# The recurrence of a hybrid transformer layer taken one direction at a time, with its input projection first

## The chip, the cores and the metric

The kernel runs on one core of a Trainium2 chip. Its engines are TensorE (PE, matmuls), VectorE (DVE), ScalarE (ACT), GpSimd (POOL) and SyncE (SP, which issues transfers); each works its own row of instructions in order, and the engines meet at semaphores. The metric is the device time of one execution in microseconds, the median of several runs.

## What is computed

Two transformer layers over 1024 latent tokens and 256 context tokens, 1024 channels wide. Layer 0 is a convolution module beside windowed attention, layer 1, which the change touches, is a bidirectional gated linear recurrence (RG-LRU) beside latent attention (MLA); a gated feed-forward follows each. Layer 1's mixer begins so:

```python
    xb_l, gt_l, cq_l, ckv_l, kr_l = split(hl @ w_in)     # recurrence, gate, query, key/value, rope key
    xb_c, gt_c, cq_c, ckv_c, kr_c = split(hc @ w_in)
    hf_l, hf_c = rglru_direction(xb_l, xb_c, ..., False) # forward
    hb_l, hb_c = rglru_direction(xb_l, xb_c, ..., True)  # backward
    c_l = ((hf_l + hb_l) * jax.nn.gelu(gt_l.astype(jnp.float32))).astype(hl.dtype)
    ...
        xc = dwconv(u, conv_w, conv_b, pad[0], pad[1])   # inside a direction: 4 taps
        r = jax.nn.sigmoid(block_diag(xc, gate_w[0], gate_b[0]).astype(jnp.float32))
        i = jax.nn.sigmoid(block_diag(xc, gate_w[1], gate_b[1]).astype(jnp.float32))
        log_a = -LRU_C * r * neg_sp
        bx = jnp.sqrt(-jnp.expm1(2.0 * log_a)) * i * xc.astype(jnp.float32)
        return jnp.exp(log_a), bx
```

Then a linear scan h = a h + bx over the context and, from its last state, over the latent tokens. `cq` and `ckv` go through an RMS norm before their own projections.

## The kernel before

Every float32 matmul is made of three passes over a high and a low part of each operand (`gemm`, L310 to 318: L315 hh x wh, L316 hl x wh, L317 hh x wl). Over 1024 input channels that is 8 k-tiles, so 24 matmuls for 128 output channels and one group of tokens: groups g0 and g1 are 512 latent tokens each, g2 the 256 context tokens. A weight tile is loaded by SyncE, its high part cast by ScalarE (L295, `wh`), its low part subtracted by GpSimd or VectorE (L298, `wl`).

The stage of the change is `proj1`, layer 1's input projections. It runs over the letters of `PROJ1` in their order: "x" projects the recurrence's input (four channel tiles on g0 and g1, then the four on g2), "c" the queries' compressed form (3 tiles), "k" the keys' and values' (2 tiles, three groups), "g" the gate branch (4 tiles, through gelu), "r" the rope key. After each gemm `pump(us)` advances the side programs in `flows` by as much of their own counting as the gemm is worth; a side program is a generator, and each `yield` of a number says for how long it rests. The order of each engine's row comes from that, and from the framework's scheduler behind it. `drain(key)` runs the side programs of one kind to their end at that place. `normed`, used by "c" and "k", starts with `drain("nrm")`, projects, and spawns a side program `fin` that takes each group's norm (matmuls with a ones vector at L436, a reciprocal root by eleven short VectorE steps L440 to 445, the diagonal `dg` at L452, a broadcast matmul at L457) and scales the columns (L1123).

The recurrence is the side program `lru` (L995 to 1065). It goes over the four channel tiles; `todo` tells it that a tile's input is written. For a tile it makes the convolution (`taps`: `xb` is read back from memory, L1013 and three L1017 for each direction, tiles of 128 x 1283), then for both directions twelve gate matmuls (L1035) with a sigmoid each (L1036), the input gate's product on GpSimd (L1038), tanh, exp and square on ScalarE (L1041, L1047, L1050), a product on VectorE (L1051), the square root on ScalarE (L1054), and then on VectorE a product (L1057) and the two scans (L1059 context, L1061 latent) of each direction. GpSimd adds the two directions (L1063) and SyncE writes the sum out (`hsd`). The numbers `LY` say how long the side program rests between these steps. ScalarE holds the tables of one set of functions; ACT_TABLE_LOAD is the change from one to another (sigmoid, exp, sqrt, gelu are in different ones here).

After `proj1` comes `mla`, the latent attention: it splits the normed columns (L321, L322), fills the constant tiles `va` and `gd` on GpSimd (L1258 to 1262), copies the rope key's tiles (L219, `kh`, `kl`, `kc`), splits the first key weights (`wk`, L1282), and starts the value gemms (L1274 to 1276) and key gemms.

Of the kernel before, what the change touches and what calls it, by code (L numbers as in the profile page):

```python
# [13 lines left out]
AF = mybir.ActivationFunctionType  # L14
ALU = mybir.AluOpType
# [10 lines left out]
TOK = (512, 512, 256)  # L26
# [34 lines left out]
PACE = 2.3  # L61
N0 = "SG"
QE0 = "VGG"
LY = (2.0, 1.0, 1.0, 2.0, 1.0, 1.0)
GY = 30.0, 4.0
DH = "s"
DL = "s"
QE00 = "GVV"
KE = "VV"
LY0 = 10.0  # L70
PROJ1 = "cxkgr"
ORD0 = "BABABABABB"

PO1 = (), ("n+++++nn",)
# [24 lines left out]
def tile_backbone(ctx: ExitStack, tc: tile.TileContext, a: dict, out: bass.AP):  # L99
    nc = tc.nc  # L100
    V, S, G, T = nc.vector, nc.scalar, nc.gpsimd, nc.tensor
    DQ = {"s": nc.sync, "a": nc.scalar, "g": nc.gpsimd}
# [20 lines left out]
    def nm(s):  # L123
        uid[0] += 1
        return f"{s}{uid[0]}"
# [10 lines left out]
    def wide():  # L136
        return psum["ca"].tile([128, 1536], F32, tag="ca", name=nm("ca"))
# [17 lines left out]
    def gate(bi, after):  # L155
        if after is not None:
            tc.add_manual_dep(bi.ins, after.ins.name, mybir.DependencyInfo(mybir.DependencyClass.NoSync, mybir.DependencyReason.DATA), reason="order")
        return bi
# [39 lines left out]
    def bank():  # L198
        return psum["mm"].tile([128, 512], F32, tag="mm", name=nm("mm"))
# [61 lines left out]
    for r, items in enumerate(rows):  # L261
        n = 0
# [17 lines left out]
    def cols(key, i, n=1):  # L280
        r, o = at[key]
        return C[:, r, o + i:o + i + n]
# [668 lines left out]
    hsd = drp.tile([128, 4, 1024], F32, name="hsd")  # L951
# [4 lines left out]
    XW = 1024 + 3 + 256  # L956
# [38 lines left out]
    def lru(todo, x5, GW, sp, tiny, done):  # L995
        def seg(t, g):
            o = OFF[g] + (3 if g == 2 else 0)
            return t[:, o:o + TOK[g]]

        def taps(i):  # L1000
            XB = x5("xb", 1)
            for o in (0, 1027, 1286):
                G.memset(XB[:, o:o + 3], 0.0)
            nc.sync.dma_start(XB[:, 3:1027], xbd[:, i, 0:1024])
            nc.sync.dma_start(XB[:, 1030:1286], xbd[:, i, 1024:1280])
            yield 3.0
            XC = []
            for d in range(2):
                x = x5("xc", 4)[:, 0:XW]
                XC.append(x)  # L1010
                tap = lambda k: cols("lcw", (d * 4 + k) * 4 + i)
                A = wide()[:, 0:XW]
                V.tensor_scalar(A, XB[:, 3:3 + XW], tap(0 if d else 3), cols("lcb", d * 4 + i), ALU.mult, ALU.add)  # L1013
                ks = (1, 2, 3) if d else (0, 1, 2)
                for k in ks:
                    o = k + 3 if d else k
                    V.scalar_tensor_tensor(x if k == ks[-1] else A, XB[:, o:o + XW], tap(k), A, ALU.mult, ALU.add)  # L1017
            return XC

        XN = None  # L1020
        for i in range(4):
            while i not in todo:
                yield 2.0
            XC = XN if XN is not None else (yield from taps(i))
            XN = None
            yield LY0 if i == 0 else LY[0]
            R, I, TT = ([x5(n, 2)[:, 0:XW] for _ in range(2)] for n in ("r", "i", "tt"))
            for d in range(2):
                x = XC[d]
                for dst in (R[d], I[d]):  # L1030
                    V.memset(dst[:, 1024:1027], 0.0)  # L1031
                for q, dst in ((0, R[d]), (1, I[d])):
                    for g in range(3):
                        ps = bank()[:, 0:TOK[g]]
                        T.matmul(ps, GW[d][:, q * 4 + i], seg(x, g), start=True, stop=True)  # L1035
                        last = S.activation(seg(dst, g), ps, AF.Sigmoid, bias=cols("lgb", (d * 2 + q) * 4 + i))  # L1036
                    yield LY[1]
                G.tensor_mul(I[d], I[d], x)  # L1038
            for d in range(2):
                c0 = d * 4 + i  # L1040
                last = gate(S.activation(TT[d], R[d], AF.Tanh, scale=sp[:, 0, c0:c0 + 1]), last)  # L1041
            if i + 1 in todo:
                XN = yield from taps(i + 1)
            yield LY[2]
            for d in range(2):
                c0 = d * 4 + i
                gate(S.activation(R[d], R[d], AF.Exp, scale=sp[:, 1, c0:c0 + 1]), last)  # L1047
            A2 = XC
            for d in range(2):
                last = S.activation(A2[d], R[d], AF.Square)  # L1050
                V.scalar_tensor_tensor(TT[d], A2[d], 1.0, TT[d], ALU.add, ALU.mult)  # L1051
            yield LY[3]
            for d in range(2):
                gate(S.activation(TT[d], TT[d], AF.Sqrt, bias=tiny), last)  # L1054
            yield LY[4]
            for d in range(2):
                V.tensor_mul(TT[d], TT[d], I[d])  # L1057
                st = (lambda t, p, q: t[:, p:q][:, ::-1]) if d else (lambda t, p, q: t[:, p:q])
                V.tensor_tensor_scan(st(A2[d], 1027, XW), st(R[d], 1027, XW), st(TT[d], 1027, XW), 0.0, ALU.mult, ALU.add)  # L1059
                init = A2[d][:, 1027:1028] if d else A2[d][:, XW - 1:XW]  # L1060
                V.tensor_tensor_scan(st(A2[d], 0, 1024), st(R[d], 0, 1024), st(TT[d], 0, 1024), init, ALU.mult, ALU.add)  # L1061
                yield LY[5]
            G.tensor_add(A2[0][:, 0:1024], A2[0][:, 0:1024], A2[1][:, 0:1024])  # L1063
            DQ[DH].dma_start(hsd[:, i], A2[0][:, 0:1024])
            done(i, "h")

    def mixer1(hs, nxt):
        pc = ph[0]
# [26 lines left out]
    def proj1(hs, w, pa, tab, KR, wv):  # L1095
# [49 lines left out]
        ready, todo = {}, set()  # L1145
        GW, sp, tiny = lru_setup(pa)
        spawn(lru(todo, x5, GW, sp, tiny, gated), "lru")
        def p_xb():
            for gs in ((0, 1), (2,)):
# [56 lines left out]

        for p in PROJ1:
            {"x": p_xb, "c": p_cq, "k": p_kv, "r": p_kr, "g": p_gt}[p]()
# [618 lines left out]
```

## Time and profile before

| | |
|---|---|
| median of 3 runs | 3096.5 us (3095.42 to 3097.85) |
| profiled execution | 3100.69 us |
| its span, first to last instruction | 3098.9 us |
| mean granted TensorE clock | 0.974 |
| TensorE busy | 2942.0 us (95%) |
| VectorE busy | 1747.0 us (56%) |
| ScalarE busy | 1093.4 us (35%) |
| GpSimd busy | 990.6 us (32%) |
| first projection gemm of layer 1 to the last | 1585.5 to 1828.9 us |

The profile holds one execution. A row of a timeline gives start and length in us, engine, line of the code, operation, the tile written and those read, and in brackets the idle time ahead of it with what ended it. TensorE's clock is given as the share of full speed that was granted.

### The profile page before, as it was taken

How to read it: one execution, taken by the hardware profiler on the slowest of the kernel's cores; microseconds unless marked ns; L12 is line 12 of the kernel's file. 1: busy time of each engine (PE TensorE's matmuls, PEld its weight loads, DVE VectorE, ACT ScalarE, POOL GpSimd, SP SyncE). 2: the span in 40 equal slices, each digit the busy share in tenths (PEclk: the TensorE clock that was granted, in tenths of full speed). 3: DMA queues.
4: the chain of work that ended last, by engine and by line, in shares of the span. 5: the costliest groups of instructions: out<-in, count | busy, mean ns of one | idle time of the engine just before them, and what ended most of it. 6: DMA issues, size and time to landing. Idle time of an engine off the chain costs nothing. (4 is left out here: it accounts for less than half of the span.)

```text
span 3098.9 us, 37481 instructions
## 1 busy us (share of the span) xinstructions
PE 2942.0 (95%) x14441; PEld 2356.5 (76%) x14441; DVE 1747.0 (56%) x2631; ACT 1093.4 (35%) x1631; POOL 990.6 (32%) x730
## 2 busy tenths in 40 slices
PE   7997899899999999999999889999998999999998
PEld 4886777778888888889997556666686888888886
DVE  4799883665654455568545986667355132232234
ACT  4213884532221112145433763333344222111213
POOL 4676546821110011055432341110253222112223
PEclk8998999999999999999999899999998999999999
DMA  8343113434442344269744230010152121111212
GB/s 295 119 129 100 37 34 111 147 101 129 139 136 82 116 144 145 88 195 281 246 155 152 94 111 26 31 38 28 57 160 89 48 62 55 34 41 55 61 41 109
DMA packets 330768, 327.04 MB, mean 106 GB/s; under 512 B 27121, under 2 KB 280734, under 8 KB 330590
## 3 DMA queue, kind: packets, MB, share of 16 engines
q1 hardware_dynamic: 326784, 321.74, 32.3%
q10 hardware_dynamic: 3806, 2.91, 0.3%
q8 instruction: 113, 1.85, 0.2%
q14 instruction: 65, 0.53, 0.1%
HBM read 255.36 MB, written 69.21 MB: 105 GB/s over the span
## 5 line engine op out<-in xcount | busy, mean ns | idle before, releaser
L298 POOL TENSOR_TENSOR wl<-wr,wh 128x1024 fp32r<-128x1024 f32 x154 | 379.9, 2468 | 1314.2 <-ACT wh L295 1283.1
L295 ACT CAST wh<-wr 128x1024 fp32r<-128x1024 f32 x248 | 259.9, 1049 | 1072.3 <-PE big L316 682.3
L315 PE MATMUL big<-hh,wh 128*128 128x512 f32 x1376 | 541.2, 394 | 4.9 <-DVE ga L1485 2.6
L316 PE MATMUL big<-hl,wh 128*128 128x512 f32 x1376 | 538.6, 392 | 3.1 <-POOL hl L503 3.1
L317 PE MATMUL big<-hh,wl 128*128 128x512 f32 x1376 | 538.8, 392 | 0.6 <-DVE wl L298 0.6
L315 PE MATMUL mm<-hh,wh 128*128 128x256 f32 (+1 forms) x1000 | 346.0, 346 | 9.6 <-DVE i L1031 9.5
L316 PE MATMUL mm<-hl,wh 128*128 128x256 f32 (+1 forms) x1000 | 339.0, 339 | 4.0 <-POOL hl L503 2.0
L317 PE MATMUL mm<-hh,wl 128*128 128x256 f32 (+1 forms) x1000 | 338.0, 338 | 3.2 <-POOL wl L298 2.5
L315 PEld LDWEIGHTS big<-hh,wh 128*128 128x128 f32 x1376 | 260.7, 190 | 61.9 <-ACT hh L498 3.4
L316 PEld LDWEIGHTS big<-hl,wh 128*128 128x128 f32 x1376 | 260.4, 189 | 58.9 <-POOL hl L503 4.3
L317 PEld LDWEIGHTS big<-hh,wl 128*128 128x128 f32 x1376 | 260.5, 189 | 55.6 <-DVE wl L298 1.0
L1553 PE MATMUL mm<-zh,wh 128*128 128x512 f32 x704 | 276.6, 393 | 1.2 <-ACT xt L1656 0.7
L1554 PE MATMUL mm<-zl,wh 128*128 128x512 f32 x704 | 275.0, 391 | 0.3 <-DVE zl L322 0.3
L1555 PE MATMUL mm<-zh,wl 128*128 128x512 f32 x704 | 275.2, 391 | 0.0
L1560 DVE TENSOR_TENSOR acc<-acc,mm 128x512 f32<-128x512 f32 x224 | 150.5, 684 | 178.7 <-PE mm L1555 178.5
L473 POOL TENSOR_TENSOR sq<-t,sq 128x512 f32<-128x512 f32 (+1 forms) x153 | 194.8, 1276 | 170.2 <-ACT t L469 152.0
L1485 DVE SCALAR_TENSOR_TENSOR ga<-big,C,ga 128x1023 f32<-128x1023 f32 x86 | 110.2, 1281 | 235.1 <-ACT ga L1498 233.8
L315 PEld LDWEIGHTS mm<-hh,wh 128*128 128x128 f32 x1000 | 192.3, 192 | 35.7 <-DVE i L1031 9.9
L316 PEld LDWEIGHTS mm<-hl,wh 128*128 128x128 f32 x1000 | 191.9, 192 | 29.4 <-POOL hl L503 5.0
L317 PEld LDWEIGHTS mm<-hh,wl 128*128 128x128 f32 x1000 | 191.6, 192 | 24.3 <-POOL wl L298 3.3
L398 DVE SCALAR_TENSOR_TENSOR wa<-wm,sc,wa 128x256 f32<-128x256 f32 x280 | 148.9, 556 | 90.4 <-DMA wm<-in_w_mod_dram 87.6
L298 DVE TENSOR_TENSOR wl<-wr,wh 128x1024 fp32r<-128x1024 f32 x94 | 131.5, 1399 | 111.6 <-ACT wh L295 108.6
(350 smaller groups left out, 5278.5 us busy)
## 6 DMA issues: line engine op xcount, KB each, us to landing
wr<-in_ffn_w_up_dram SPq DMA_DIRECT2D x132, 512.0 KB, 4.3
wm<-in_w_mod_dram SPq DMA_DIRECT2D x224, 128.0 KB, 2.2
wr<-in_ffn_w_down_dram SPq DMA_DIRECT2D x44, 512.0 KB, 3.5
wm<-in_w_mod_dram SPq DMA_DIRECT2D x40, 512.0 KB, 6.5
xd<-x SPq DMA_DIRECT2D x38, 512.0 KB, 4.1
x<-xd SPq DMA_DIRECT2D x38, 512.0 KB, 6.6
wr<-in_ab_w_out_dram SPq DMA_DIRECT2D x24, 512.0 KB, 7.2
wdd<-wh SPq DMA_DIRECT2D x22, 512.0 KB, 2.6
```

What stands on the lines that cost most here:

```text
L295: S.copy(hi[:, 0:nk, 0:m], raw[:, 0:nk, 0:m])
L298: (G if e[wn[0] % len(e)] == "G" else V).tensor_sub(lo[:, 0:nk, 0:m], raw[:, 0:nk, 0:m], f32(hi[:, 0:nk, 0:m]))
L315: T.matmul(ps, wh, xh[k], start=i == 0, stop=False)
L316: T.matmul(ps, wh, xl[k], start=False, stop=False)
L317: T.matmul(ps, wl, xh[k], start=False, stop=i == n - 1)
L398: V.scalar_tensor_tensor(acc[:, v], raw, sc[:, k, v:v + 1], acc[:, v], ALU.mult, ALU.add)
L473: self.eng.tensor_add(self.acc[-1], t, self.acc[-1])
L1485: V.scalar_tensor_tensor(dst[:, lo:hi], src[:, lo + d - o:hi + d - o], k, dst[:, lo:hi], ALU.mult, ALU.add)
L1553: T.matmul(ps, wh, zh, start=j == j0, stop=False)
L1554: T.matmul(ps, wh, zl, start=False, stop=False)
L1555: T.matmul(ps, wl, zh, start=False, stop=j == j1 - 1)
L1560: V.tensor_add(ys[g][c], ys[g][c], ps)
```

## The change

The unit of `lru` becomes one direction of one channel tile: eight units u, tile u // 2, direction u % 2. `gates(u)` holds the gate matmuls, sigmoids, GpSimd's product and the tanh of a unit; `ahead(i)` the taps of a tile. Unit u goes exp, square, product, then the gates of unit u + 1, then its square root, product and scans. `r`, `i` and `tt` still have two buffers, which are now those of two units, not of two directions. GpSimd's add and the write follow each second unit. `LY` gets new numbers, and `PROJ1` puts x ahead of c: "xckgr".

```diff
-LY = (2.0, 1.0, 1.0, 2.0, 1.0, 1.0)
+LY = (2.0, 2.0, 1.0, 2.0, 3.0, 3.0)
...
-PROJ1 = "cxkgr"
+PROJ1 = "xckgr"
...
-            for d in range(2):
-                c0 = d * 4 + i
-                last = gate(S.activation(TT[d], R[d], AF.Tanh, scale=sp[:, 0, c0:c0 + 1]), last)
-            if i + 1 in todo:
-                XN = yield from taps(i + 1)
-            yield LY[2]
-            for d in range(2):
-                c0 = d * 4 + i
-                gate(S.activation(R[d], R[d], AF.Exp, scale=sp[:, 1, c0:c0 + 1]), last)
-            A2 = XC
-            for d in range(2):
-                last = S.activation(A2[d], R[d], AF.Square)
-                V.scalar_tensor_tensor(TT[d], A2[d], 1.0, TT[d], ALU.add, ALU.mult)
-            yield LY[3]
-            for d in range(2):
-                gate(S.activation(TT[d], TT[d], AF.Sqrt, bias=tiny), last)
...
+        def gates(u):
+            i, d = u // 2, u % 2
+            R, I, TT = RI[u] = [x5(n, 2)[:, 0:XW] for n in ("r", "i", "tt")]
+            x, c0 = XC[i][d], d * 4 + i
+            for q, dst in ((0, R), (1, I)):
+                V.memset(dst[:, 1024:1027], 0.0)
+                for g in range(3):
+                    ps = bank()[:, 0:TOK[g]]
+                    T.matmul(ps, GW[d][:, q * 4 + i], seg(x, g), start=True, stop=True)
+                    last[0] = gate(S.activation(seg(dst, g), ps, AF.Sigmoid, bias=cols("lgb", (d * 2 + q) * 4 + i)), last[0] if g == q == 0 else None)
+                yield LY[1]
+            G.tensor_mul(I, I, x)
+            last[0] = S.activation(TT, R, AF.Tanh, scale=sp[:, 0, c0:c0 + 1])
...
+        yield from ahead(0)
+        yield LY0
+        yield from gates(0)
+        for u in range(8):
+            i, d = u // 2, u % 2
+            (R, I, TT), A2, c0 = RI[u], XC[i][d], d * 4 + i
+            gate(S.activation(R, R, AF.Exp, scale=sp[:, 1, c0:c0 + 1]), last[0])
+            last[0] = S.activation(A2, R, AF.Square)
+            V.scalar_tensor_tensor(TT, A2, 1.0, TT, ALU.add, ALU.mult)
+            yield LY[0]
+            if u < 7:
+                yield from gates(u + 1)
+            last[0] = gate(S.activation(TT, TT, AF.Sqrt, bias=tiny), last[0])
             yield LY[4]
...
+            if d:
+                h = XC[i][0][:, 0:1024]
+                G.tensor_add(h, h, A2[:, 0:1024])
+                DQ[DH].dma_start(hsd[:, i], h)
+                done(i, "h")
+            elif i < 3:
+                yield from ahead(i + 1)
```

`gate(x, y)` only puts x behind y in the order of their engine. Lines behind L1066 stand 3 further on in the changed kernel, and lines inside `lru` have new numbers: the gate matmul is L1031, its sigmoid L1032, the product on GpSimd L1034, tanh L1035, exp L1048, square L1049, VectorE's products L1050 and L1056, the square root L1054, the scans L1058 and L1060, GpSimd's add L1064. The number of instructions is the same on every engine but ScalarE, which has 14 more table loads (40 instead of 26).

TensorE, at the norms of c. Before (the norm of c's g0, between two gemms of x; `mm_14014` and `dg_14029` are the context norm):

```order
L317 MATMUL mm_13989<-hh_11736,wl_13986 128x512
L436 MATMUL mm_14014<-ones,sq_13863 128x1 x2
L436 MATMUL mm_14031<-ones,sq_13747 128x1 x4
L315 MATMUL mm_14053<-hh_12595,wh_13985 128x512
...
L317 MATMUL mm_14053<-hh_12598,wl_13986 128x512
L457 MATMUL mm_14078<-dg_14029,ones 128x256
L457 MATMUL mm_14093<-dg_14048,ones 128x512
L315 MATMUL mm_14116<-hh_11733,wh_14112 128x512
```

After (both norms of c, ahead of k's first gemm `mm_14617`):

```order
L1031 MATMUL mm_14533<-xc_14470,gw_13668 128x512
L1031 MATMUL mm_14536<-xc_14470,gw_13668 128x256
L436 MATMUL mm_14545<-ones,sq_14276 128x1 x4
L457 MATMUL mm_14564<-dg_14562,ones 128x512
L436 MATMUL mm_14578<-ones,sq_14334 128x1 x4
L457 MATMUL mm_14597<-dg_14595,ones 128x512
L315 MATMUL mm_14617<-hh_11733,wh_14613 128x512
```

Before, a gemm of 24 matmuls stands between a norm's column sums and its broadcast; after, none does for c's norms. For k's first norm (`dg_14944`) one gemm and three gate matmuls stand there after.

VectorE, the steps of such a norm up to its `dg`. Before (k's first norm, among g's gemms, the one that TensorE waits for in rows 3 below):

```order
L445 SCALAR_TENSOR_TENSOR rst_14899<-mm_14894,rst_14899 128x4
L1013 TENSOR_SCALAR ca_15080<-xb_15073,C 128x1283
L1051 SCALAR_TENSOR_TENSOR tt_14756<-xc_14693,tt_14756 128x1283
L1051 SCALAR_TENSOR_TENSOR tt_14757<-xc_14699,tt_14757 128x1283
L443 TENSOR_TENSOR mm_14894<-mm_14894,rst_14899 128x4
L1017 SCALAR_TENSOR_TENSOR ca_15080<-xb_15073,C,ca_15080 128x1283
L444 SCALAR_TENSOR_TENSOR mm_14894<-mm_14894,rst_14899 128x4
L1017 SCALAR_TENSOR_TENSOR ca_15080<-xb_15073,C,ca_15080 128x1283
L445 SCALAR_TENSOR_TENSOR rst_14899<-mm_14894,rst_14899 128x4
L1057 TENSOR_TENSOR tt_14756<-tt_14756,i_14754 128x1283
L452 TENSOR_TENSOR dg_14911<-ident,rst_14899 128x512
```

After (c's second norm; `xc_14815` takes over a buffer that GpSimd's add of tile 0 reads):

```order
L440 TENSOR_SCALAR mm_14578<-mm_14578 128x4
L1056 TENSOR_TENSOR tt_14369<-tt_14369,i_14368 128x1283
...
L1058 SCALAR_TENSOR_TENSOR xc_14199<-r_14367,tt_14369 128x256
...
L1060 SCALAR_TENSOR_TENSOR xc_14199<-r_14367,xc_14199,tt_14369 128x1024
...
L1050 SCALAR_TENSOR_TENSOR tt_14518<-xc_14470,tt_14518 128x1283
...
L1017 SCALAR_TENSOR_TENSOR xc_14815<-xb_14809,C,ca_14816 128x1283
...
L1013 TENSOR_SCALAR ca_14822<-xb_14809,C 128x1283
...
L1017 SCALAR_TENSOR_TENSOR ca_14822<-xb_14809,C,ca_14822 128x1283
L443 TENSOR_TENSOR mm_14578<-mm_14578,rst_14583 128x4
L1017 SCALAR_TENSOR_TENSOR ca_14822<-xb_14809,C,ca_14822 128x1283
L444 SCALAR_TENSOR_TENSOR mm_14578<-mm_14578,rst_14583 128x4
L1017 SCALAR_TENSOR_TENSOR xc_14821<-xb_14809,C,ca_14822 128x1283
L445 SCALAR_TENSOR_TENSOR rst_14583<-mm_14578,rst_14583 128x4
L452 TENSOR_TENSOR dg_14595<-ident,rst_14583 128x512
```

Between the first step and `dg` stand six long operations of the recurrence before (one of them, L1013, behind eight steps in a row), and nine after, a scan of 1024 columns among them. Ahead of the after's L440 stand the three products of c's first norm (L1126).

GpSimd, from the last add of the recurrence to the key weights `wk`. Before:

```order
L1063 TENSOR_TENSOR xc_15079<-xc_15079,xc_15085 128x1024
L1258 MEMSET va 128x4x64 x10
L1261 MEMSET gd 128x128
L219 TENSOR_SCALAR kc_15529<-kc_15522 64x512
L219 TENSOR_SCALAR kc_15535<-kc_15522 64x512
L1262 MEMSET gd 1x128
L1282 TENSOR_TENSOR wk_15603<-wr_15597,wk_15602 128x256
```

After:

```order
L1064 TENSOR_TENSOR xc_15139<-xc_15139,xc_15145 128x1024
L219 TENSOR_SCALAR kh_15527<-kh_15520 64x1024
L219 TENSOR_SCALAR kl_15528<-kl_15521 64x1024
L219 TENSOR_SCALAR kh_15533<-kh_15520 64x1024
L219 TENSOR_SCALAR kl_15534<-kl_15521 64x1024
L219 TENSOR_SCALAR kc_15529<-kc_15522 64x512
L219 TENSOR_SCALAR kc_15535<-kc_15522 64x512
L1261 MEMSET va 128x4x64 x10
L1264 MEMSET gd 128x128
L1285 TENSOR_TENSOR wk_15603<-wr_15597,wk_15602 128x256
```

Four copies of 64 x 1024 have moved ahead of `wk`. On VectorE the last unit's scans now stand among the steps of r's rope (L1187 to 1191), behind r's gemms.

## Rows read from the trace of the kernel before

**Rows 1.** Stretches: length, busy us per engine (instructions), granted clock, DMA share, GB/s.

```profile
1585.50:1682.00 96.50, 94.45 (x469) 78.89 (x467) 50.51 (x135) 28.65 (x53) 36.44 (x34) 1.00 0.47 149
1682.00:1829.00 147.00, 129.03 (x528) 95.53 (x528) 127.82 (x131) 103.40 (x118) 53.19 (x45) 0.94 0.30 97
...
1727.00:1732.00 5.00, 5.00 (x26) 4.62 (x26) 4.81 (x5) 1.02 (x2) 2.74 (x2) 0.67 0.40 157
...
1756.00:1765.00 9.00, 9.00 (x28) 6.28 (x27) 9.00 (x5) 1.10 (x2) 3.55 (x1) 0.72 0.36 113
```

**Rows 2.** TensorE's waits, 1585.5 to 1829: us in total, times, longest.

```profile
PE mm L315 <- DVE i L1031: 9.5, 1, 9.5
PE mm L457 <- DVE dg L452: 5.8, 1, 5.8
PE mm L1035 <- ACT r L1036: 2.6, 2, 1.4
```

**Rows 3.** Timeline of VectorE at both waits, and the matmul that waits.

```profile
1721.47 4.56 DVE L1061 TENSOR_TENSOR_SCAN xc<-r,xc,tt 128x1024 f32<-128x1024 f32 x2
...
1744.24 0.17 DVE L440 TENSOR_SCALAR mm<-mm 128x4 f32<-128x4 f32 x1 [3.36 <-PE mm L436]
...
1747.29 2.89 DVE L1051 SCALAR_TENSOR_TENSOR tt<-xc,tt 128x1283 f32<-128x1283 f32 x2
...
1754.70 0.68 DVE L452 TENSOR_TENSOR dg<-ident,rst 128x512 f32<-128x512 f32 x1
...
1755.53 2.05 PE L457 MATMUL mm<-dg,ones 128*128 128x512 f32 x2 [5.79 <-DVE dg L452]
```

**Rows 4.** Timeline of VectorE and GpSimd, the context norm (L496, L503).

```profile
1632.41 0.87 DVE L496 SCALAR_TENSOR_TENSOR t<-x,MOD,mm 128x256 f32<-128x256 f32 x2 [2.93 <-PE mm L457]
...
1636.19 0.69 DVE L1157 COPY t<-mm 128x512 f32<-128x512 f32 x1 [0.63 <-POOL hl L503]
...
1641.10 0.48 DVE L496 SCALAR_TENSOR_TENSOR t<-x,MOD,mm 128x256 f32<-128x256 f32 x1 [1.99 <-DMA cqd<-t]
...
1644.78 1.72 POOL L503 TENSOR_TENSOR hl<-t,hh 128x256 fp32r<-128x256 f32 x2 [0.76 <-ACT hh L502]
```

**Rows 5.** Timeline of TensorE (a tile's gates) and of ScalarE (a table load).

```profile
1692.56 8.76 PE L1035 MATMUL mm<-xc,gw 128*128 128x512 f32 x24
...
1701.86 2.62 ACT L1041 ACTIVATE tt<-r,sp 128x1283 f32<-128x1283 f32 x2
1704.50 1.28 ACT L1047 ACT_TABLE_LOAD   x1
```

**Rows 6.** VectorE's groups, 1682 to 1829: busy us, mean ns, idle before.

```profile
L1017 DVE SCALAR_TENSOR_TENSOR ca<-xb,C,ca 128x1283 f32<-128x1283 f32 x16 | 24.9, 1556 | 0.5
...
L1057 DVE TENSOR_TENSOR tt<-tt,i 128x1283 f32<-128x1283 f32 x8 | 11.6, 1485 | 1.7 <-ACT tt L1054 1.7
...
L1123 DVE SCALAR_TENSOR_TENSOR t<-t,C,mm 128x512 f32<-128x512 f32 x4 | 2.8, 731 | 0.7 <-PE mm L457 0.7
```

**Rows 7.** Timeline of VectorE, GpSimd and TensorE at the handover to the attention.

```profile
1821.87 4.57 DVE L1061 TENSOR_TENSOR_SCAN xc<-r,xc,tt 128x1024 f32<-128x1024 f32 x2
...
1826.61 2.68 POOL L1063 TENSOR_TENSOR xc<-xc,xc 128x1024 f32<-128x1024 f32 x1 [17.62 <-DVE xc L1061]
1832.19 2.58 POOL L1258 MEMSET va<- 128x256 f32 x10 [2.90 <-DMA hsd<-xc]
...
1835.01 1.63 POOL L219 TENSOR_SCALAR kc<-kc 64x512 fp32r<-64x512 f32 x2
...
1838.67 0.73 POOL L1282 TENSOR_TENSOR wk<-wr,wk 128x256 fp32r<-128x256 f32 x1 [1.77 <-ACT wk L1281]
...
1847.35 1.56 POOL L219 TENSOR_SCALAR kl<-kl 64x1024 fp32r<-64x1024 f32 x1
...
1835.32 0.79 PE L1274 MATMUL mm<-wh,kvh 128*128 128x512 f32 x1 [6.40 <-ACT kvh L321]
...
1846.91 0.76 PE L1274 MATMUL mm<-wh,kvh 128*128 128x512 f32 x1 [4.85 <-DVE kl L1307]
```

More of the change, by code (lines that the diff above doesn't have):

```diff
@@ L1018, in taps @@
             return XC
-        XN = None
-        for i in range(4):
+        XC, RI, last = {}, {}, [None]
+        def gates(u):
[11 more added lines that the diff above has]
+            last[0] = S.activation(TT, R, AF.Tanh, scale=sp[:, 0, c0:c0 + 1])
@@ L1022, in lru, with ahead @@
+        def ahead(i):
             while i not in todo:
                 yield 2.0
[L1024 to L1027, printed above, removed]
-            for d in range(2):
[L1029 to L1038, printed above, removed]
@@ L1052, in lru @@
-            yield LY[3]
-            for d in range(2):
-                gate(S.activation(TT[d], TT[d], AF.Sqrt, bias=tiny), last)
-            yield LY[4]
[L1056 to L1062, printed above, removed]
@@ L1063, in lru @@
-            G.tensor_add(A2[0][:, 0:1024], A2[0][:, 0:1024], A2[1][:, 0:1024])
-            DQ[DH].dma_start(hsd[:, i], A2[0][:, 0:1024])
-            done(i, "h")
+            XC[i] = yield from taps(i)
+        yield from ahead(0)
[11 more added lines that the diff above has]
+            last[0] = gate(S.activation(TT, TT, AF.Sqrt, bias=tiny), last[0])
+            yield LY[4]
+            V.tensor_mul(TT, TT, I)
+            st = (lambda t, p, q: t[:, p:q][:, ::-1]) if d else (lambda t, p, q: t[:, p:q])
+            V.tensor_tensor_scan(st(A2, 1027, XW), st(R, 1027, XW), st(TT, 1027, XW), 0.0, ALU.mult, ALU.add)
+            init = A2[:, 1027:1028] if d else A2[:, XW - 1:XW]
+            V.tensor_tensor_scan(st(A2, 0, 1024), st(R, 0, 1024), st(TT, 0, 1024), init, ALU.mult, ALU.add)
+            yield LY[5]
+            if d:
[5 more added lines that the diff above has]
+                yield from ahead(i + 1)
```

## The prediction

> **What bounds the kernel now.** TensorE is busy for 95% of the span, so only the stage that the change touches was read: layer 1's input projections, with the recurrence woven in. First the stretches [rows 1]: up to 1682 us (c, x and their context gemms) TensorE works 94.45 of 96.5 us; from 1682 to 1829 (k, g, r beside the recurrence) 129.03 of 147 us, at a granted clock of 0.94. VectorE is busy there for 127.82 us and ScalarE for 103.40. So three engines are nearly full and TensorE is idle for 2.05 + 17.97 = 20.0 us.
>
> Next, who ends its waits [rows 2]. The longest, 9.5 us, ends with a memset of a few columns (L1031), the next, 5.8 us, with the diagonal tile `dg` that a norm's broadcast multiplies (L452). Neither is costly; they stand late in VectorE's row, as its own timeline tells [rows 3]: ahead of the memsets two long scans run from 1721.47 for 4.56 us, and the steps of the norm that make `dg` begin at 1744.24 with 0.17 us each, but `dg` is written only at 1754.70, because long operations of the recurrence stand between them. TensorE had one gemm there, and finished it at 1755.53 - 5.79 = 1749.74. A gemm of 24 matmuls over 512 columns is thus about 5.5 us.
>
> After such a pause the clock is low [rows 1]: 0.67 in 1727 to 1732 (26 records in 5.0 us; at half the price of 512 columns they would be about 3.1, so 1.9 lost) and 0.72 in 1756 to 1765 (28 records in 9.0 us against 28 x 0.23 = 6.4, so 2.6 lost). **Losses of the stage before: 20.0 + 1.9 + 2.6 = 24.5 us.** The sum is the losses after minus these, since matmuls and VectorE's work stay the same, plus what changes where the next stage takes over.
>
> **The change part by part.** *x first.* c's six gemms (6 x 5.5 = 33 us) move behind x, so the taps, which start once x's first context gemm is in, start that much earlier. That takes away the place in which both scans of a tile stood ahead of the memsets, and the 9.5 us with it; all of the 24.5 is given back before new losses are counted.
>
> *Term A, the context norm.* The norm of the context tokens now has x's eight gemms ahead of its use, and no c. In the trace it runs from 1632.41 to the end of its last pieces at 1644.78 + 1.72 = 1646.5, 14.1 us; 4.9 of these (1636.19 to 1641.10) went to c's columns and their DMA [rows 4]. That leaves 9.2 us. The first pair of context gemms is woven matmul by matmul and covers at most 2 x 2.75 = 5.5. The rest, 3.7, and the last matmuls behind it: 5 us, between 2 (the norm gets ahead under x) and 10 (nothing is covered).
>
> *Term B, ScalarE ahead of the gates.* By going unit by unit, ScalarE changes between sigmoid, sqrt and exp eight times instead of four: 14 more table loads. One load is 1.28 us, begun 0.02 us behind the activation ahead of it [rows 5]: 14 x 1.28 = 18 us of work on an engine that was idle for 43.6 of 147 us. Only what a gate matmul waits for counts, as its bank is freed by a sigmoid. The gates waited 2.6 us in four tiles [rows 2]; with a set of loads at each of eight units I take twice that, 5.2, and two loads at g, where gelu and sigmoid now alternate gemm by gemm: 2.6. Together 8 us; bounds 2.6 (as before) and 5.2 + 18 = 23 (every added load is waited for).
>
> The trace shows no pause between an activation and a load. The Trainium skill ("ScalarE: Activation LUTs", section "What ACT_TABLE_LOAD costs") puts a drain of about 1380 ns beside the 1283 ns of the load, and advises under "Table sets: the hidden batching unit" to batch calls by set, which is the opposite of this change. The load agrees with the trace, the drain does not show there; by the page's 2.66 us the 14 loads would be 37 us of ScalarE and B's upper bound 42, by the row they are 18 and it is 23.
>
> *Term C, c's norms.* This is the largest. `normed` begins by draining "nrm". Before, c's norms trickled out under x's gemms. Now k follows c at once, so both of c's norms stand between c's last gemm and k's first, with no gemm between, as the rows of TensorE's order show. First norm: eleven steps of 0.17 us and `dg` at 0.68 [rows 3], with gaps 2.9 us of waiting. Second: VectorE has three products of 0.73 (2.2) ahead of it [rows 6], and in between nine long operations: a product of 1.49, the scan 2.28 and its context part (256 of 1024 columns, an estimate of 0.6), 1.45 (half of 2.89), and five tap operations at 1.556 = 7.8 [rows 3, 6]. These are 13.6. One tap operation waits for GpSimd's add of the tile just scanned, 2.7 us [rows 7] against 1.45 of work in between: 1.2. With `dg` 0.7 and 0.3 of steps: 18.0. So 2.9 + 18.0 = 21 us, between 18 (overlaps, GpSimd in time) and 24 (slower scans). The clock then falls as at 1756: 2.6 (1.9 to 2.6). A wait of a kind that cost 5.8 before has become one three times as long. It cannot be hidden: each engine works its rows in their order, and TensorE has nothing else there.
>
> *Term D, k's first norm.* Here a gemm and three gate matmuls (8.76 / 12 x 3 = 2.2 us, [rows 5]) stand between. Against the 5.8 us place, VectorE has some 1.5 us more of long work and 0.7 fewer steps in a row, TensorE 2.2 more to do, and a tap operation waits 1.6 us for GpSimd's add behind a scan: 5.8 + 1.5 - 0.7 - 2.2 + 1.6 = 6 us, 4.4 to 9, and 2.6 for the clock (0 to 2.6).
>
> Sum: A 5 + B 8 + C 23.6 + D 8.6 = 45.2 against 24.5: the last projection gemm ends **20.7 us later**.
>
> *The handover.* Before, the last scan ended at 1821.87 + 4.57 = 1826.4, 2.5 us ahead of the last gemm (1828.9), and GpSimd's `wk`, for which the key gemms wait, was ready at 1838.67 + 0.73 = 1839.4 [rows 7]. Now unit 7's scan comes some 3.5 us behind the last gemm, 1853, and GpSimd has the add (2.7), six copies (four at 1.56 and 1.63 for two: 7.9), the memsets of `va` (2.6) and `wk` (0.7) behind it, 0.5 for gaps: 1867.4, or 28.0 later, 7.3 more than the gemms. Against that VectorE arrives without a backlog, and the wait of 4.8 us for `kl` [rows 7] goes. Net +2.5; bounds -5 (no copy is waited for) and +8.
>
> In all 20.7 + 2.5 = 23.2 us. The profiled execution took 3100.7 us, so 3123.9; it lies 4.2 above the median of the runs, 3096.5, and it is the median that I forecast: **3119.7, say 3120**. All lower bounds: A 2, B 2.6, C 19.9, D 4.4 = 28.9, +4.4 against 24.5, -0.6 with the handover: 3096. All upper: 10 + 23 + 26.6 + 11.6 = 71.2, +46.7, with 8 it is +55: 3151.
>
> **The rivals.** *ScalarE becomes the bound:* all 14 loads lie in front of gates. B is 23 instead of 8, the time 3135. For it: ScalarE was 70% busy in the stage, and would carry 18 us more in a stretch of about the same length, shared by gates and gelus. Against: before, no wait for ScalarE was above 1.4 us [rows 2], and the recurrence has 33 us more to run in.
>
> *Not slower:* finer units and an early start leave VectorE and ScalarE ahead of TensorE everywhere that order allows. A and B are 0, C and D at their low ends (19.9 + 4.4 = 24.3, as much as the stage lost before), and the handover is at -5: 3091 to 3096, within 0.2% or just below. It decides by the last scan: if that ends before 1826, this is it. For it: VectorE sat idle for 19 of 147 us. The Trainium skill ("Perfetto Trace Analysis", section "Optimizing Scalar/DVE Operations") says it as a rule: where Scalar and Vector aren't saturated but cause bubbles elsewhere, breaking up instructions may let work complete sooner; that the bubbles here came from VectorE's order agrees [rows 2, 3]. Against: C is fixed by the order.
>
> *Only the certain part:* C and D as summed, A and B at their low ends, no change at the handover: 2 + 2.6 + 23.6 + 8.6 - 24.5 = +12.3: 3109.
>
> **How the numbers follow.** Forecast, about 3112 to 3130: 0.50. Only the certain part, 3103 to 3112: 0.18. ScalarE as the bound, 3130 to 3150: 0.14. Not slower, 3085 to 3103: 0.18. The range of 8 in 10 leaves out the lower half of the last case and the upper half of ScalarE's: 3097 to 3138. A measurement of this kernel tells 0.2%, 6.2 us, from no change. Of the last case 0.06 lie below 3090.3 and 0.12 between there and 3102.7; the others are slower: 0.82.
>
> **What would show it.** C is right if TensorE's longest wait is one of some 17 to 18 us for `dg` with the start of k behind it, and a low clock after; D if a second one of about 6 us ends with `dg`. B: waits of the gates for ScalarE sum to 5 to 10 us, with 14 more loads of 1.28 us. A: waits for the context's pieces of some 5 us at the end of x. The last gemm of r ends near 1850, the last scan behind it, `wk` near 1867. The forecast is wrong if the wait for c's norms is under 10 us, if gates wait over 15 us, or if TensorE works on while GpSimd copies.

## The result and the profile after

The changed kernel takes 3136.46 us (median of 4 runs, 3132.93 to 3139.98) against 3097.18 us before: 1.0122 times as long, 95% interval 1.0110 to 1.0135. That is 39.3 us more, where 23 were forecast; the time lies at the upper end of the range. The profiled execution has a span of 3138.2 us and a mean granted clock of 0.966.

The stretches of the same stage after (columns as in [rows 1]):

```profile
1585.50:1682.00 96.50, 92.18 (x437) 74.61 (x436) 59.64 (x117) 43.04 (x72) 34.00 (x35) 0.98 0.39 118
1682.00:1829.00 147.00, 112.29 (x450) 83.38 (x449) 90.27 (x123) 86.99 (x95) 45.32 (x42) 0.86 0.29 95
...
1700.00:1702.00 2.00, 1.78 (x4) 1.01 (x5) 1.30 (x2) 0.61 (x1) 0.00 (x0) 0.90 0.35 131
1702.00:1704.00 2.00, 2.00 (x7) 1.33 (x6) 0.00 (x0) 1.18 (x4) 0.00 (x0) 0.50 0.69 197
1704.00:1730.00 26.00, 4.58 (x15) 3.40 (x15) 20.18 (x38) 8.39 (x8) 7.85 (x6) 0.50 0.33 116
1730.00:1736.00 6.00, 5.66 (x12) 3.83 (x13) 3.77 (x5) 0.00 (x0) 0.00 (x0) 0.52 0.71 236
1736.00:1740.00 4.00, 4.00 (x20) 3.29 (x19) 3.63 (x4) 0.00 (x0) 0.00 (x0) 1.00 0.02 7
```

In the same 147 us TensorE does 112.29 us of work instead of 129.03, at a clock of 0.86 instead of 0.94, and VectorE does 90.27 instead of 127.82: nobody is full any more, and the stage is long because of a hole, 1704 to 1730, in which TensorE works 4.6 of 26 us at half clock.

TensorE's waits from the first to the last projection gemm, 1585.5 to 1860 (the four lines left out have 2.8 us):

```profile
PE mm L457 <- DVE dg L452: 28.3, 3, 17.9
PE mm L1031 <- DVE t L1113: 3.8, 1, 3.8
PE mm L315 <- ACT i L1032: 1.8, 1, 1.8
PE mm L316 <- DVE hl L499: 1.5, 1, 1.5
PE mm L315 <- ACT hh L498: 1.2, 1, 1.2
PE mm L1031 <- ACT r L1032: 1.1, 3, 0.5
```

The wait of 9.5 us in [rows 2] is gone. The one of 5.8 us, for the diagonal `dg` of k's first norm, is still there, and with two new ones of its kind it makes 28.3 us. Where the three lie, from TensorE's timeline:

```profile
1700.22 3.32 PE L1031 MATMUL mm<-xc,gw 128*128 128x512 f32 x6 [3.83 <-DVE t L1113]
1703.34 1.70 PE L436 MATMUL mm<-ones,sq 128*128 128x1 f32 x8
1708.94 2.04 PE L457 MATMUL mm<-dg,ones 128*128 128x512 f32 x2 [3.91 <-DVE dg L452]
1710.78 1.71 PE L436 MATMUL mm<-ones,sq 128*128 128x1 f32 x8
1730.34 2.04 PE L457 MATMUL mm<-dg,ones 128*128 128x512 f32 x2 [17.86 <-DVE dg L452]
...
1792.03 2.05 PE L457 MATMUL mm<-dg,ones 128*128 128x512 f32 x2 [6.49 <-DVE dg L452]
```

The first two waits for `dg` are c's norms ahead of k, 3.91 and 17.86 us; the third is k's first norm, 6.49. What VectorE does during the long one:

```profile
1713.07 0.16 DVE L440 TENSOR_SCALAR mm<-mm 128x4 f32<-128x4 f32 x1
1713.14 1.48 DVE L1056 TENSOR_TENSOR tt<-tt,i 128x1283 f32<-128x1283 f32 x1
...
1715.39 2.35 DVE L1060 TENSOR_TENSOR_SCAN xc<-r,xc,tt 128x1024 f32<-128x1024 f32 x1
...
1721.42 1.55 DVE L1017 SCALAR_TENSOR_TENSOR xc<-xb,C,ca 128x1283 f32<-128x1283 f32 x1 [1.95 <-POOL xc L1064]
...
1729.51 0.69 DVE L452 TENSOR_TENSOR dg<-ident,rst 128x512 f32<-128x512 f32 x1
```

From the first step of the norm (0.16 us) to `dg` it is 16.4 us. Nine long operations of the recurrence fill 13.9 of them, a scan among them, and 1.95 more go to a tap operation's wait for GpSimd's add.

The other place is the handover to the attention. Rows of VectorE, ScalarE, GpSimd and TensorE there, which answer to [rows 7]:

```profile
1855.15 2.35 DVE L1060 TENSOR_TENSOR_SCAN xc<-r,xc,tt 128x1024 f32<-128x1024 f32 x1
...
1858.25 1.50 DVE L1050 SCALAR_TENSOR_TENSOR tt<-xc,tt 128x1283 f32<-128x1283 f32 x1
...
1865.60 2.34 DVE L1060 TENSOR_TENSOR_SCAN xc<-r,xc,tt 128x1024 f32<-128x1024 f32 x1
...
1859.78 1.36 ACT L1054 ACTIVATE tt<-tt,tiny 128x1283 f32<-128x1283 f32 x1 [3.66 <-DVE tt L1050]
...
1875.31 0.40 ACT L321 CAST kc<-kr 64x256 fp32r<-64x256 f32 x1 [6.05 <-DMA hsd<-xc]
1875.74 0.41 ACT L1284 CAST wk<-wr 128x256 fp32r<-128x256 f32 x1
...
1868.12 3.88 POOL L1064 TENSOR_TENSOR xc<-xc,xc 128x1024 f32<-128x1024 f32 x1 [18.24 <-DVE xc L1060]
1872.09 1.90 POOL L219 TENSOR_SCALAR kh<-kh 64x1024 fp32r<-64x1024 f32 x1
...
1882.39 0.72 POOL L1285 TENSOR_TENSOR wk<-wr,wk 128x256 fp32r<-128x256 f32 x1
...
1861.71 0.55 PE L1277 MATMUL mm<-wh,kvh 128*128 128x512 f32 x1 [2.01 <-ACT kvh L321]
...
1876.24 0.77 PE L315 MATMUL mm<-kvh,wk 128*128 128x512 f32 x1 [9.61 <-ACT wk L1284]
...
1883.17 0.80 PE L317 MATMUL mm<-kvh,wk 128*128 128x512 f32 x1 [4.88 <-POOL wk L1285]
```

The projections end at 1861.71 - 2.01 = 1859.7. Unit 6's scan has ended only 2.2 us ahead of that, unit 7's square root waits 3.66 us for a product behind that scan, and its own scan ends at 1867.9. GpSimd's add, the copies and `va` follow, and `wk` is whole at 1883.1. TensorE waits 9.61 us for the high half of `wk` (on ScalarE, whose cast ahead of it waits 6.05 us for the write of the recurrence's last sum) and 4.88 us for the low half.

So that other kernels can be compared, here are two lengths of each profile. The *stage* runs from the start of the first projection gemm to the end of TensorE's last projection work (k's last norm, or the last gates, where these come last); the *handover* from there to the end of the last value matmul of `v_all`. Before: 1585.49 to 1828.9 and on to 1876.8. After: 1587.92 to 1859.7 and on to 1914.8. That is 28.4 us more in the stage and 7.2 in the handover; 1.3 come later, and 2.4 lie ahead of the stage, where the code is the same (in the fourteen profiles the first gemm starts between 1581.9 and 1590.4).

### The profile page after: what moved, and what is told of

Same layout as the page of the kernel before. It is cut to its first block, busy times and chain, and to the rows that moved or that the text cites. A ratio compares the mean times of both kernels' runs of the same rounds, so it can differ in the third digit from the quotient of the medians.

```text
span 3138.2 us, 37480 instructions
## 1 busy us (share of the span) xinstructions
PE 2951.1 (94%) x14441; PEld 2362.1 (75%) x14441; DVE 1733.5 (55%) x2631; ACT 1113.5 (35%) x1645; POOL 989.5 (32%) x730
## 4 chain that ended last, share of the span: by engine, by line
PE 77%; DVE 9%; issue 3%; POOL 3%; DMA 3%; ACT 3%; SPq 0%; ACTq 0%; POOLq 0%; DVEq 0%
PE big L315 10%; PE big L317 9%; PE big L316 9%; PE mm L315 6%; PE mm L316 6%; PE mm L317 6%; PE mm L1556 5%; PE mm L1557 5%; PE mm L1558 5%; PE po L1387 3%; POOL sq L473 1%; PE mm L899 1%; PE mm L906 1%; DMA wr<-in_ffn_w_up_dram 1%; PE sx L1339 1%
## 5 line engine op out<-in xcount | busy, mean ns | idle before, releaser
L298 POOL TENSOR_TENSOR wl<-wr,wh 128x1024 fp32r<-128x1024 f32 x154 | 380.0, 2468 | 1285.5 <-ACT wh L295 1254.2
L298 DVE TENSOR_TENSOR wl<-wr,wh 128x1024 fp32r<-128x1024 f32 x94 | 131.2, 1396 | 104.3 <-ACT wh L295 100.5
```

The lines of the kernel that those rows point to most:

```text
L298: (G if e[wn[0] % len(e)] == "G" else V).tensor_sub(lo[:, 0:nk, 0:m], raw[:, 0:nk, 0:m], f32(hi[:, 0:nk, 0:m]))
```

## The experiments

Theory 1: the loss is made by the order, c's two norms between c and k, and by a tail of the recurrence that ends behind r. Theory 2: the units themselves make it, by more table loads and gates that wait for ScalarE. Times are medians; the ratio is to the kernel before in the same set of runs, with its 95% interval.

| kernel | us | ratio (interval) | stage | handover |
|---|---|---|---|---|
| before (c, x; both directions) | 3097.2 | 1 | 243.4 | 47.9 |
| after (x, c; units) | 3136.5 | 1.0122 (1.0110 to 1.0135) | 271.8 | 55.1 |
| e1: units, c first | 3123.0 | 1.0077 (1.0062 to 1.0092) | 249.3 | 64.2 |
| e2: x first, both directions | 3126.9 | 1.0089 (1.0074 to 1.0105) | 275.6 | 43.2 |
| e4: after, no square root | 3131.9 | 1.0105 (1.0090 to 1.0120) | 267.1 | 57.2 |
| e7: after, old rests | 3131.4 | 1.0096 (1.0078 to 1.0114) | 277.8 | 41.5 |
| e8: after, r between c and k | 3126.5 | 1.0090 (1.0075 to 1.0105) | 257.9 | 54.7 |
| e9: as e8, old rests | 3137.5 | 1.0130 (1.0114 to 1.0147) | 265.3 | 50.4 |
| e10: before, x, c, r, k, g | 3124.4 | 1.0089 (1.0072 to 1.0106) | 262.7 | 49.9 |
| e11: units, c first, old rests | 3112.3 | 1.0042 (1.0027 to 1.0057) | 251.8 | 47.8 |
| e12: units, c first, short rests | 3122.2 | 1.0076 (1.0058 to 1.0094) | 270.9 | 43.7 |
| e13: after without c's norms | 3108.2 | 1.0030 (1.0020 to 1.0040) | 242.9 | 57.6 |
| e14: before without c's norms | 3094.3 | 0.9987 (0.9977 to 0.9998) | 239.3 | 45.4 |
| e16: before, copies on ScalarE | 3093.8 | 0.9989 (0.9980 to 0.9997) | 240.1 | 44.8 |

**c's norms taken out, in both kernels.**

```diff
-            spawn(fin(), "nrm")
+            if key != "qn":
+                spawn(fin(), "nrm")
```

> The changed kernel without the norm of c's columns (c goes on unnormed, so the queries are not the reference's; the sums, the reciprocal root, the broadcast and six products with their transfers are left out). Theory: with it the waits of 3.9 and 17.9 us and the half clock behind them go, 24 to 30 us in all: 3106 to 3113 us. If what VectorE still has to do only makes TensorE wait elsewhere: 3122 to 3132 us.

> The same left out of the kernel before, where the norms of c run under x's gemms: by the theory they cost next to nothing there, 3088 to 3098 us. If the norms cost by their own work and not by their place, some 25 us less here too: 3070 to 3080 us.

The changed kernel gives back 28.3 us, nearly three quarters of its loss, and its stage is then as long as that of before (242.9 and 243.4). In the kernel before the same work costs 0.6 to 7 us (0.9977 to 0.9998). Both times lie in the ranges of the theory. So of the 28.3 us some 21 to 28 are the place of the norms and not their work: shown. In the profile of e13 the hole is gone and the other waits stand as in after:

```profile
1696.44 4.64 PE L1031 MATMUL mm<-xc,gw 128*128 128x512 f32 x6 [3.83 <-DVE t L1113]
...
1759.62 2.04 PE L457 MATMUL mm<-dg,ones 128*128 128x512 f32 x2 [6.50 <-DVE dg L452]
...
1843.18 0.77 PE L315 MATMUL mm<-kvh,wk 128*128 128x512 f32 x1 [9.53 <-ACT wk L1285]
...
1850.21 0.80 PE L317 MATMUL mm<-kvh,wk 128*128 128x512 f32 x1 [4.98 <-POOL wk L1286]
```

What is left, 1.0030, is the handover: 57.6 us against 47.9 before.

**The order alone, and the units alone.**

```diff
-PROJ1 = "cxkgr"      # e2: in the kernel before
+PROJ1 = "xckgr"
...
-PROJ1 = "xckgr"      # e1: in the changed kernel
+PROJ1 = "cxkgr"
```

> The kernel before with x's projection ahead of c's, and nothing else: both directions of a tile still go together. Theory 1: a wait of 15 to 20 us for c's second norm shows ahead of k, as in the changed kernel, and with it the time is 3100 to 3115 us, since the two waits of before (9.5 and 5.8 us) go and the recurrence ends early. Theory 2: no loss without the units, 3085 to 3097 us.

> The changed kernel with c's projection ahead of x again (the loop over the side programs goes over a copy of their list, since one is now added while it runs). Theory 1, the loss lies in the two norms of c that stand between c and k with no gemm (3.9 and 17.9 us of waiting in the trace after, and a half clock behind): the 17.9 us wait is gone, and what is left is the units' own: 3105 to 3122 us, of which up to 10 for a tail that ends later, since the recurrence starts 33 us later. Theory 2, the units by themselves cost it (14 more table loads, gates that wait for ScalarE): 3130 to 3140 us.

The order alone costs 28.8 us, more than I expected, and theory 2 falls with it as the only cause. TensorE in e2:

```profile
1695.16 8.13 PE L1035 MATMUL mm<-xc,gw 128*128 128x512 f32 x18 [7.63 <-ACT r L1036]
...
1722.86 2.05 PE L457 MATMUL mm<-dg,ones 128*128 128x512 f32 x2 [13.33 <-DVE dg L452]
...
1741.45 2.07 PE L457 MATMUL mm<-dg,ones 128*128 128x512 f32 x2 [15.04 <-DVE dg L452]
```

Both norms wait nearly as long as the second does in after (13.33 and 15.04 us against 17.86), and the gates of the second tile wait 7.63 us more. With units two are in flight and that wait shrinks: on top of the order the units are worth a little in the stage (275.6 to 271.8, one profile each) and cost in the handover (43.2 to 55.1).

The units alone cost 25.0 us, 1 us above the range of theory 1, and hardly in the stage (249.3): the handover is 64.2 us long. In e1 the recurrence starts late and its last gates stand behind r. Rows of TensorE and, last, VectorE:

```profile
1830.34 2.96 PE L1031 MATMUL mm<-xc,gw 128*128 128x512 f32 x4 [6.50 <-ACT i L1032]
1841.09 0.80 PE L1277 MATMUL mm<-wh,kvh 128*128 128x512 f32 x1 [7.78 <-ACT kvh L321]
...
1860.33 0.76 PE L315 MATMUL mm<-kvh,wk 128*128 128x512 f32 x1 [14.15 <-ACT wk L1284]
...
1849.20 3.12 DVE L1060 TENSOR_TENSOR_SCAN xc<-r,xc,tt 128x1024 f32<-128x1024 f32 x1
```

So either part alone loses, each by another mechanism, and together they don't add up: with x first the recurrence ends earlier, and the units' tail is 9 us shorter.

**The tail, by the rests.** `LY` is set to that of the kernel before, in the changed kernel (e7) and with c first (e11).

```diff
-LY = (2.0, 2.0, 1.0, 2.0, 3.0, 3.0)
+LY = (2.0, 1.0, 1.0, 2.0, 1.0, 1.0)
```

> The changed kernel with the rests LY of the kernel before (2, 1, 1, 2, 1, 1), so that the units follow each other more closely and the last one ends among g's gemms instead of behind r. Theory 1 with a tail: c's wait of 18 us stays, the handover (last scan 8 us behind the last gemm, key weights at 1883) is given back, some 10 to 20 us: 3116 to 3127 us. If the tail is hidden anyway: 3133 to 3140 us. If the closer units crowd ScalarE: above 3140.

> Units of one direction, c ahead of x, and the rests LY of the kernel before: of the change only the units are left. If the loss with c first (3123 us) was the tail, a last scan 19 us behind the last gemm, it is given back, as the last gates now stand ahead of g's last gemm: 3098 to 3110 us. If the units themselves cost it (42 table loads, gates that wait for ScalarE): 3117 to 3128 us.

The tail goes: the last scan of e7 stands at 1824.62, over 40 us ahead of the last gemm, and its handover is 41.5 us instead of 55.1. But the stage grows by 6.0, since TensorE now waits 11.8 us for ScalarE's sigmoids, and the net gain is 5.0 us, the two intervals just overlapping; the time lies between the first two ranges expected. With c first (e11) the gain is 10.7 us, the clearer case, but this time too lies between its two ranges. The handover is there as short as before (47.8 and 47.9), and e11 is still 13.6 us slower than before: the stage is 8.4 us longer, with waits of TensorE for ScalarE's sigmoids and gelus of 13.2 us in sum (2.6 before), and 6.2 us more come behind the handover. So the tail is what makes the handover long: shown. Shorter rests don't win it for nothing; they trade it for waits for ScalarE, which is the mechanism of theory 2. Halving the rests once more settles that:

```diff
+LY = (1.0, 0.5, 1.0, 1.0, 0.5, 0.5)   # e12: units, c first
```

> Units of one direction with c first and rests of half the old length (1, 0.5, 1, 1, 0.5, 0.5), so that the last gates stand among g's first gemms. If what is left of the units' cost with the old rests (3112 us) is a recurrence that ends late and GpSimd's add behind it, 3098 to 3108 us; if closer units make more gates wait for ScalarE and more gemms for VectorE, 3112 to 3125 us.

The second expectation held: the handover is the shortest with c first (43.7), and the stage is 19 us longer than in e11. TensorE waits in many places, longest here:

```profile
1751.24 2.07 PE L1031 MATMUL mm<-xc,gw 128*128 128x512 f32 x2 [5.69 <-DVE t L1113]
...
1795.62 0.80 PE L315 MATMUL mm<-hh,wh 128*128 128x512 f32 x1 [7.42 <-ACT wh L295]
```

The second is a weight's cast that stands on ScalarE behind sigmoids, a tanh, a square root, an exp and their table loads.

**The table loads.**

```diff
-last[0] = gate(S.activation(TT, TT, AF.Sqrt, bias=tiny), last[0])
+last[0] = gate(S.activation(TT, TT, AF.Square), last[0])
```

> The changed kernel with the square root of the recurrence replaced by a square, which leaves the root's value out of the result and takes 8 of the 40 table loads away (some 10 us of ScalarE). Theory 1: the loads lie beside other work, 3130 to 3138 us. Theory 2, ScalarE bounds the stage: 3122 to 3128 us.

Eight loads fewer bring 4.6 us, with intervals that overlap a little (1.0090 to 1.0120 against 1.0110 to 1.0135). That lies in the range of theory 1, and is under half of the 10 us that the loads last. A part of them may lie on the path, not all; more than that this run doesn't settle.

**A cover for c's norms.** r's three gemms go between c and k ("xcrkg"), in the changed kernel (e8), with the old rests (e9) and in the kernel before (e10).

> The changed kernel with r's three gemms between c and k and g last (xcrkg). c's first norm now has a gemm and six gate matmuls between its sums and its broadcast, the second still none. If c's norms cost what stands between them on VectorE while TensorE has nothing, the wait goes from 21.8 to 8 to 14 us in sum, and the time to 3112 to 3126 us; if the order of VectorE keeps the whole wait, 3132 to 3140 us.

> As the run before with the old rests: the recurrence ends among g's gemms. c's wait 8 to 14 us and no tail: 3100 to 3118 us. If gates that wait for ScalarE take it back, as they did with the old rests before: 3120 to 3130 us.

> The kernel before with the order xcrkg, both directions of a tile together. By the theory of c's norms its two waits (13.3 and 15.0 us with xckgr) fall to 8 to 16 us in sum: 3105 to 3118 us. If x first costs by something else (gates and scans that meet c's gemms), 3122 to 3130 us.

e8 is 10 us faster than after, just above the range expected: c's norms wait 3.53 and 11.16 us, 14.7 instead of 8 to 14:

```profile
1721.17 1.90 PE L457 MATMUL mm<-dg,ones 128*128 128x512 f32 x2 [3.53 <-DVE dg L452]
1738.67 2.08 PE L457 MATMUL mm<-dg,ones 128*128 128x512 f32 x2 [11.16 <-DVE dg L452]
```

The other two are no better. e9 lies above both of its ranges. e10 lies in its second one, in which x first costs by something else: the norms' waits do fall from 28.4 to 7 us, and the time by 2.4 only. Its TensorE:

```profile
1692.24 9.12 PE L1035 MATMUL mm<-xc,gw 128*128 128x512 f32 x18 [7.67 <-ACT r L1036]
...
1724.15 0.80 PE L315 MATMUL mm<-hh,wh 128*128 128x512 f32 x1 [8.93 <-ACT r L1036]
...
1741.79 2.05 PE L457 MATMUL mm<-dg,ones 128*128 128x512 f32 x2 [1.06 <-DVE dg L452]
1753.95 2.07 PE L457 MATMUL mm<-dg,ones 128*128 128x512 f32 x2 [5.93 <-DVE dg L452]
```

A new wait of 8.93 us takes the place of the old: ScalarE's sigmoid of the third tile there waits for VectorE's scan of an earlier one, and r's gemm for the bank. In e9 one wait for `dg` is still 16.8 us. These kernels also lose 5.5 to 8.5 us more than before behind the handover. g comes last there, so that the gating products fall into the attention; but e11, where g keeps its place, loses 6.2 us there too, so why stays open. So a gemm as cover takes waits of the norms away, but with x first the recurrence and c, r or k want VectorE at the same time, and the wait turns up elsewhere. Why e9 is slower than e8 by 11 us stays open: the profiled execution of e9, at 3130 us the fastest of its four, shows only part of it.

**The wait of before.** [rows 2] put 9.5 us down to a memset. In the same row of VectorE, behind the two scans, stands a copy of k's columns out of PSUM, which frees a bank. Those copies on ScalarE:

```diff
-                    V.tensor_copy(t, ps)      # in normed
+                    S.copy(t, ps)
```

> The kernel before with the copies of c's and k's columns out of PSUM (L1110) on ScalarE instead of VectorE. The wait of 9.5 us in the trace before ends with VectorE's row of 1725.98, where such a copy stands with the memsets behind two scans; if the copy that frees the bank is its cause, it goes, with the half clock behind it: 3084 to 3093 us. If ScalarE, between sigmoids and table loads, is as late as VectorE: 3095 to 3106 us.

The wait of 9.5 us is gone and that of 5.8 is down to 0.75; new ones for sigmoids, 10.7 us in sum, take most of it back:

```profile
1721.59 4.97 PE L1035 MATMUL mm<-xc,gw 128*128 128x512 f32 x8 [3.34 <-ACT r L1036]
...
1754.93 7.33 PE L1035 MATMUL mm<-xc,gw 128*128 128x512 f32 x15 [3.61 <-ACT r L1036]
...
1787.50 8.83 PE L1035 MATMUL mm<-xc,gw 128*128 128x512 f32 x16 [3.38 <-ACT r L1036]
```

The time lies just above the first range expected. The ratio is 0.9989 (0.9980 to 0.9997), some 3.4 us: the one kernel here that leaves nothing out and beats both, by little. It also shows that the memset of [rows 2] was not what TensorE waited for; the copy was. In e16 the same context gemm follows the same gates and starts at 1712.69, 0.48 us of waiting behind them, while the memsets still stand behind the two scans, at 1723.00:

```profile
1712.69 0.39 PE L315 MATMUL mm<-hh,wh 128*128 128x256 f32 x1 [0.48 <-ACT t L1110]
```

## Why the prediction was right, and where its sizes were off

**The sign and the place were right.** The sum of TensorE's waits in the stage was forecast at A 5 + B 8 + C 21 + D 6 = 40 us, and is 40.5; that it fits so closely is luck, since its parts don't. Term C, 2.9 + 18.0 us, is 3.91 + 17.86. The working by VectorE's row holds for each long operation; the first norm's `dg` took 1.44 us instead of 0.68, and the tap operation waits 1.95 us instead of 1.2, as GpSimd's add took 3.57 instead of 2.7. Term D, 6 us, is 6.49. Term A, 5 us, is 1.2 + 1.5 and some 0.7 for weights, 3.4 in all.

**B was too large and hid a miss.** TensorE waits for ScalarE's sigmoids and gelus 3.4 us, not 8 (1.8 + 1.1 + 0.5). A wait that I didn't have fills the sum up: 3.83 us for a copy out of PSUM (L1113) that stands on VectorE behind tap operations, ahead of c's norms. The time lies outside the band of the forecast itself, 3112 to 3130, and inside the whole range only by the share that the rival with ScalarE as the bound put into it. That rival gave 3135 us, next to the measured 3136.5, by a mechanism that the waits of this kernel and e4 speak against. So the range held by luck, and a time that fits is no proof of its rival.

**The clock was mis-sized.** The stage grew by 28.4 us, its waits by 20.7 (40.5 - 19.8); the other 7.7 are work that ran more slowly, where the sum has 5.2 - 4.5 = 0.7. I counted the gemm behind each of two pauses. But the granted clock is 0.90 in 1700 to 1702, 0.50 from there to 1730 and 0.52 to 1736, and what TensorE does in all that time is slow, from the gates at 1700 on and the small matmuls too. It is low again behind the wait at 1792 (0.54 and 0.60 in the 8 us from 1790) and at x's context gemms (0.59 in 1636 to 1640). Six gates take 3.32 us instead of 2.31 (1.0), the sums at L436 1.70 and 1.71 instead of 0.95 (1.5), three broadcasts some 2.04 instead of some 1.02 (3.0), two gemms 8.07 and 7.96 instead of 5.61 (4.8), and a pair of context gemms 1.8 more: 12.1 us. Counted in the same way the kernel before has 5.3 (a gemm 2.5, a broadcast 1.0, a context gemm 1.8), where the sum had 4.5. The difference is 6.8 us; 0.9 of the 7.7 stay unplaced. With its clock C costs 27.8 by these rows (21.8 of waits, 6.0 of slow work), where the sum had 23.6. The 28.3 us of e13 are not the same thing: they hold the norms' own work too, and without the norms the gates ahead of them are the slower (4.64 us instead of 3.32).

**The handover was mis-sized.** Forecast +2.5, measured 7.2 + 1.3 = 8.5. The step that failed is the 3.5 us from the last gemm to the last scan: it is 8.2, because units 6 and 7 are both still on their way, and unit 7's product and square root stand behind unit 6's scan. The add took 3.9 instead of 2.7. So `wk` is whole 23.4 us behind the last gemm, not 17.8. What I had not seen is ScalarE: a cast of `kc` waits for the write of the last sum, and the high half of `wk` stands behind it.

Together: 28.4 - 20.7 = 7.7 us of the stage and 6.0 of the handover were missing, 13.7, and 2.4 us of the profiled execution lie ahead of the stage.

**Two rules and the runs.** The Trainium skill's rule to batch activations by table set ("ScalarE: Activation LUTs", section "Table sets: the hidden batching unit") speaks against the change, and the change lost, but only in small part by that: without eight of the loads e4 is 4.6 us faster. In the changed kernel too a load of 1.28 us begins where the activation ahead of it ends (1846.72 + 1.38, the load at 1848.11); no drain shows. The Trainium skill also says that breaking up instructions may let work complete sooner where Scalar or Vector cause bubbles on other engines ("Perfetto Trace Analysis", section "Optimizing Scalar/DVE Operations"). The runs don't bear that out here: with units the stage is 3.8 us shorter where x is first (e2 to after) and 5.9 us longer where c is (before to e1), and the whole kernel is slower both times. It didn't help where the order of an engine's row, and not the length of an operation, made the bubble.

## What to carry to other kernels

A step with a round trip (TensorE, then a chain of short VectorE steps, then TensorE) cost little more than its own work while independent gemms stood between its ends (0.6 to 7 us for c's norms), and all that VectorE's row held when none did. Here a drain at the head of the next stage put c's norms there, so look for one first when stages change places; no run took the drain itself away. Price a pause with the half clock in and behind it, down to the small matmuls. When a side program is cut finer, see where its last piece ends: here what the next stage needed stood behind that piece on VectorE, ScalarE and GpSimd. Packing the pieces closer moved that cost into waits for ScalarE.

## What the runs showed of the hardware

The granted clock was 0.50 in all of 1704 to 1730, where TensorE worked 4.6 of 26 us, 0.52 from 1730 to 1736, where it was busy again for 5.7 of 6 us, and 1.00 from 1736: the level is 1.2 GHz through the pause and for some 5 us of full work behind it, then 2.4 GHz. In the handover after it was 0.50 from 1865 to 1890.

GpSimd and VectorE are slower together in some places: GpSimd's add of 128 x 1024 took 3.88 us where VectorE was at `kvl` and `kl`, 3.57 where VectorE was at a product of 128 x 1283 (1717.82), 2.40 and 2.42 at the two other tiles of the changed kernel, and 2.68 before [rows 7]. The subtraction of `kl` on VectorE beside it took 3.25 us, and 1.22 in the profile before, where GpSimd was at a copy of 64 x 1024. A subtraction of 128 x 1024 on VectorE (L298) took 8.10 us before, beside an add and products on GpSimd (1801.96), and 1.22 after, where GpSimd was idle (1700.08). Why is not shown by these runs.
